# The first norm's factor moved behind the matmul: v from a raw, already transposed x

## The chip, the cores and the metric

One core of a Trainium2 chip runs the whole kernel. The metric is device time in microseconds (us) of one execution; the time before is the median of three runs. A difference under about 0.2% of it (2.4 us) is not told from no change.

## The reference

Two layers of a decoder trunk run over 512 tokens of 1024 channels in float32. Each layer is a mixer, a squared-ReLU MLP and a gated embedding, with an RMSNorm ahead of each and behind each. Layer 0 mixes by attention with a forget gate, layer 1 by a short convolution. The change touches only the beginning of layer 0:

```python
hn   = x * rsqrt(mean(x*x, axis=-1) + 1e-6) * g        # RMSNorm, one factor per token
proj = hn @ w_attn_in                                  # q | k | v | forget-gate logits
log_f = log_sigmoid(proj[..., 3*D:] + b_forget)
c     = cumsum(log_f, axis=1)
s     = q @ k.T / 8 + c[:, None] - c[None, :]          # causal, softmax over keys
m     = softmax(s) @ v @ w_attn_out
```

The factor `r = rsqrt(...)` belongs to a token, and a token is a row of `hn` and of `proj`. So `(x * r) @ w` and `(x @ w) * r` are the same product.

## The kernel before, in words

Every float32 operand of a matmul is split into a high part (rounded to the fast matmul format) and a low part (the rest). A product is then three matmuls: high by high, low by high, high by low (`mm3`, lines 266 to 272). The gain `g` of the first norm is multiplied into the rows of the weights while these are split (`split_gained`, L279: ScalarE writes the high part at L285, VectorE the low part at L287). `prepare(n)` splits weight tiles up to the n-th in a planned order and fetches what it needs into 14 buffers; `wide(...)` calls it eight tiles ahead of the matmul that wants one. Split weights, x and most other blocks are tiles of 128 x 512 in one pool of 70 "pages"; matmul results take one of eight banks of PSUM.

The tokens stand in four blocks t of 128. For attention the norm's result must stand as channels (on the partitions) by tokens, in the pair `hT`. It is made so, for each block: two DMAs load x as tokens by channels (`load_x`); ScalarE and VectorE take the mean square of one half each (L312, L317), GpSimd raises it to the power -1/2 (L692), VectorE multiplies (L698, `n_h`), TensorE turns 2 x 4 squares by a transpose (L337, `n_p`), ScalarE and VectorE split the turned block into `hT` (L276 and L277, for block 0 L723 and L708).

v and the 16 gate logits are made in three column chunks, `V_CHUNKS`: chunk 0 is 272 columns wide (256 of v and the 16 logits), chunk 1 is 512 and chunk 2 is 256. `values(c, t)` makes one chunk of one block with 24 matmuls (8 slices of channels, three matmuls each). Chunk 0 runs by an order written out by hand (`manual_schedule`, lines 716 to 748): twelve matmuls on a constant tile come first (`work(12)`, L1152), and the transposes of the next block stand in the midst of each block's 24 matmuls (L479). Chunks 1 and 2 (L472, with the matmuls at L268 to L270) and everything after have their order set by a planner, that may also place such work between the steps written by hand. `keep_v` adds the gate bias to the logits and splits v out of PSUM (ScalarE L500, VectorE L502). Then come the logs of the gates, their running sum by matmul (`sums_of_logs`, L446, put behind chunk 1 of block 2), its way through DRAM to the score biases (L459, L550), chunk 2, and the projection of q and k from all of `hT` (`project`, from the first matmul on all 512 tokens at once).

All loads go through SyncE's queue in order, apart from half of the first x block and the gains, that go through ScalarE's. The first loads have their order written by hand (lines 1139 to 1147): x block 0, four weight tiles, x block 1, four weight tiles, x blocks 2 and 3, the gate bias.

Of the kernel before, what the change touches and what calls it, by code (L numbers as in the profile page):

```python
# [8 lines left out]
F32 = mybir.dt.float32  # L9
# [6 lines left out]
P = 128  # L16
D = 1024
# [51 lines left out]
def trunk(ctx: ExitStack, tc, x, pT, g, gT, wv, wqk, bf, wo, wci, wcq, cw, wco, wup, wdn, wpp, wpg, out):  # L69
# [308 lines left out]
    def load_x(name, t):  # L378
        xs = [page(f"{name}{t}_{n}") for n in range(2)]
        for n in range(2):  # L380
            eng = nc.scalar if name == "xa" and n else nc.sync
            eng.dma_start(xs[n][:, :S], x[t * P : (t + 1) * P, n * S : (n + 1) * S])
        return xs
# [29 lines left out]
    def attention(hT, first_x, b_f, work, by_hand):  # L413
        vs = [[page(f"v{t}_{i}", F32R) for i in range(4)] for t in range(NB)]
# [46 lines left out]
        def values(c, t, mid=None):  # L461

            c0, width = V_CHUNKS[c]
            n_v = min(width, D - c0)
            ps = bank(f"v{c}_{t}")
            for k in range(KT):
                if width == 256:
                    w = wide("v", c, k // 2).at(lambda u: u[:, k % 2 * 256 : k % 2 * 256 + 256])
                else:
                    w = wide("v", c, k, soon=0 if mid else SOON)  # L470
                if not mid:
                    mm3(ps[:, :width], tokens(hT, k, t), w, k == 0, k == KT - 1)  # L472
            HH, LH, HL = ("hi", "hi"), ("lo", "hi"), ("hi", "lo")
            order = [(u, n) for n in range(2) for u in (HH, HL, LH)] if mid else []
            for i, ((part, of), n) in enumerate(order):
                if i == (5 if t else 3):
                    mid()
                for k in range(4 * n, 4 * n + 4):
                    nc.tensor.matmul(  # L479
                        ps[:, :width], getattr(tokens(hT, k, t), part),  # L480
                        getattr(ready["v", c, k], of),
                        start=k == 0 and part == of, stop=k == KT - 1 and part == "lo",
                    )

            def keep_v():
                if n_v < width:
                    nc.vector.tensor_tensor(
                        out=logit[:, t * H : (t + 1) * H], in0=ps[:, n_v:width], in1=b_f,
                        op=ALU.add,
                    )  # L490
                splits = []
                for c1 in range(0, n_v, 256):
                    src = ps[:, c1 : c1 + 256].rearrange("p (i e d) -> p i e d", e=2, d=HD)
                    block = vs[t][(c0 + c1) // 256].rearrange("p (i r) -> p i r", i=2)
                    for e in range(2):
                        hi = block[:, :, 192 * e : 192 * e + HD]
                        lo = block[:, :, 64 + 64 * e : 128 + 64 * e]
                        splits.append((hi, lo, src[:, :, e, :]))
                for hi, _, src in splits:
                    nc.scalar.copy(hi, src)  # L500
                for hi, lo, src in splits:
# [3 lines left out]

            return keep_v
# [174 lines left out]
        E, done_v = mybir.EngineType, []  # L681
# [13 lines left out]
        def scale_rows(t, r):  # L695
            hs = [page(f"{name}_h{t}_{n}") for n in range(2)]
            for n in range(2):
                nc.vector.tensor_scalar(  # L698
                    out=hs[n][:, :S], in0=first_x[t][n][:, :S], scalar1=r, scalar2=None,
                    op0=ALU.mult,  # L700
                )
            return hs

        quads = lambda ps: ps.rearrange("p (j c) -> p j c", j=4)

        def keep_low(n, ps):
            hi, lo = (u[:, 4 * n : 4 * n + 4, :P] for u in (hT.hi, hT.lo))
            nc.vector.tensor_tensor(  # L708
                out=lo, in0=quads(ps), in1=hi.bitcast(F32), op=ALU.subtract
            )  # L710

        def turn_rows(t, hs):
            for n in range(2):
                keep(t, n, turned(t, n, hs[n], name), hT)

        with tc.manual_schedule(engines={E.PE, E.DVE, E.Activation, E.Pool}):
            work(12)
            r = inverse(0, mean_squares(0))
            prepare(2)
            hs = scale_rows(0, r)  # L720
            prepare(4)
            ps0 = [turned(0, n, hs[n], name) for n in range(2)]
            nc.scalar.copy(hT.hi[:, :4, :P], quads(ps0[0]))  # L723
            v = mean_squares(1)
            keep_low(0, ps0[0])
            prepare(5)
            r = inverse(1, v)
            nc.scalar.copy(hT.hi[:, 4:, :P], quads(ps0[1]))
            hs1 = scale_rows(1, r)
            prepare(KT)  # L730
            keep_low(1, ps0[1])
            v = mean_squares(2)
            r = inverse(2, v)
            done_v.append(values(0, 0, lambda: turn_rows(1, hs1)))
# [545 lines left out]
```

## Time and profile before

| | us |
|---|---|
| median of 3 runs | 1221.15 |
| lowest, highest | 1221.05, 1221.59 |
| the profiled execution | 1220.75 |
| its span, first to last instruction | 1219.0 |
| TensorE busy | 1208.5 |
| VectorE busy | 919.2 |
| ScalarE busy | 684.0 |
| GpSimd busy | 653.8 |
| read from HBM | 136.93 MB |

In rows of the profile PE is TensorE's matmuls, PEld its weight loads, DVE VectorE, ACT ScalarE, POOL GpSimd, SP SyncE; a q behind a name is that engine's queue of DMA issues and waits. A timeline row holds the start, the time from the first start to the last end, engine, line, operation, tiles (written <- read), and a count where like instructions in a row are merged. Matmuls overlap: the distance of two starts, not the length of one, is what one costs. A group's row holds busy time and the mean of one in ns. A table by windows gives each engine's busy time in each stretch.

### The profile page before, as it was taken

The page shows a single profiled execution, that of the slowest core. Times are in us where ns is not written, and L with a number is a line of the kernel's source. Part 1 is how long each engine was busy: PE and PEld are TensorE (multiplying, and loading weights), DVE is VectorE, ACT ScalarE, POOL GpSimd, SP SyncE. Part 2 cuts the span into 40 slices and gives each one's busy share as a digit, 9 for nine tenths or more (in the row PEclk, how much of TensorE's full clock was granted, in tenths as well). Part 3 has the DMA queues.
Part 4 walks back from the last instruction along what each step waited for, and adds up shares of the span by engine and source line. Part 5 has one row for each costly group of instructions (what it writes and reads, how often), then busy time and mean ns, then how long its engine had stood idle before and what let it go on. Part 6 is the DMA issues. An engine that isn't in the chain of part 4 may idle for free.

```text
span 1219.0 us, 18773 instructions
## 1 busy us (share of the span) xinstructions
PE 1208.5 (99%) x6202; PEld 1030.3 (85%) x6202; DVE 919.2 (75%) x1466; ACT 684.0 (56%) x1457; POOL 653.8 (54%) x612
## 2 busy tenths in 40 slices
PE   9999999999999999999999999999999999999997
PEld 7888887898888888888889999989888888888886
DVE  7668889576769766879877788766876787669873
ACT  5567778458634563455666433545756445635551
POOL 1036667154787777775213355226676878678210
PEclk9999999999999999999999999999999999999999
DMA  8555555623244223438223123552422443235401
GB/s 277 168 151 164 166 142 134 216 88 95 87 121 138 87 73 119 138 88 284 73 91 114 28 86 104 164 164 70 138 84 60 134 139 100 64 113 176 169 12 58
DMA packets 86162, 148.74 MB, mean 122 GB/s; under 512 B 10224, under 2 KB 17952, under 8 KB 86064
## 3 DMA queue, kind: packets, MB, share of 16 engines
q1 hardware_dynamic: 85488, 147.01, 39.3%
q8 instruction: 49, 0.80, 0.3%
q10 hardware_dynamic: 576, 0.53, 0.1%
q14 instruction: 49, 0.40, 0.1%
HBM read 136.93 MB, written 6.37 MB: 118 GB/s over the span
## 4 chain that ended last, share of the span: by engine, by line
PE 92%; issue 2%; DVE 2%; ACT 2%; POOL 1%; DMA 0%; POOLq 0%; DVEq 0%; ACTq 0%
PE up L268 9%; PE up L270 9%; PE up L269 9%; PE dn L268 8%; PE dn L270 8%; PE dn L269 8%; PE qk L270 2%; PE qk L269 2%; PE qk L268 2%; PE pg L268 2%; PE pg L270 2%; PE pg L269 2%; PE pT L579 1%; PE co L269 1%; PE co L268 1%
## 5 line engine op out<-in xcount | busy, mean ns | idle before, releaser
L277 DVE TENSOR_TENSOR wl<-raw,wh 128x512 fp32r<-128x512 f32 x346 | 344.8, 1042 | 14.4 <-ACT wh L276 13.5
L269 PE MATMUL up<-hTh,wl 128*128 128x512 f32 (+1 forms) x576 | 210.2, 365 | 0.0
L270 PE MATMUL up<-hTl,wh 128*128 128x512 f32 (+1 forms) x576 | 209.6, 365 | 0.0
L268 PE MATMUL up<-hTh,wh 128*128 128x512 f32 (+1 forms) x576 | 208.7, 366 | 0.0
L276 ACT CAST wh<-raw 128x512 fp32r<-128x512 f32 x346 | 189.8, 626 | 4.5 <-DVE xd L373 4.4
L940 ACT ACTIVATE r<-up 128x512 f32<-128x512 f32 (+1 forms) x72 | 39.6, 550 | 202.2 <-PE up L270 180.9
L277 POOL TENSOR_TENSOR wl<-dn_T,wh 128x512 fp32r<-128x512 f32 x96 | 132.1, 1410 | 30.1 <-ACT wh L276 30.1
L168 POOL TENSOR_TENSOR dn_T<-raw,raw 128x512 f32<-128x512 f32 x56 | 87.3, 1570 | 69.1 <-DMA raw<-in_wdn 49.1
L269 PEld LDWEIGHTS up<-hTh,wl 128*128 128x128 f32 x576 | 108.6, 188 | 17.5
L268 PEld LDWEIGHTS up<-hTh,wh 128*128 128x128 f32 x576 | 108.6, 188 | 17.5
L270 PEld LDWEIGHTS up<-hTl,wh 128*128 128x128 f32 x576 | 108.2, 188 | 17.6
L986 DVE TENSOR_TENSOR acc<-dn,acc 128x512 f32<-128x512 f32 x168 | 107.4, 679 | 14.9 <-PE dn L270 14.8
L168 POOL TENSOR_TENSOR dn_T<-raw,dn_T 128x512 f32<-128x512 f32 x56 | 92.3, 1648 | 2.2
L276 ACT CAST wh<-dn_T 128x512 fp32r<-128x512 f32 x112 | 61.5, 618 | 10.9 <-POOL dn_T L168 10.9
L277 DVE TENSOR_TENSOR A12l<-q,A12h 128x512 fp32r<-128x512 f32 x28 | 22.0, 787 | 53.9 <-ACT A12h L276 53.9
L1000 POOL TENSOR_TENSOR acc<-acc,acc 128x512 f32<-128x512 f32 x28 | 46.9, 1708 | 9.9 <-DVE acc L986 9.9
L270 PE MATMUL qk<-hTl,wh 128*128 128x512 f32 x128 | 50.8, 397 | 0.0
L269 PE MATMUL qk<-hTh,wl 128*128 128x512 f32 x128 | 50.8, 397 | 0.0
L268 PE MATMUL qk<-hTh,wh 128*128 128x512 f32 x128 | 50.7, 396 | 0.0
L269 PE MATMUL pg<-wh,hTl 128*128 128x512 f32 x128 | 50.5, 394 | 0.0
L268 PE MATMUL pg<-wh,hTh 128*128 128x512 f32 x128 | 50.4, 394 | 0.0
L270 PE MATMUL pg<-wl,hTh 128*128 128x512 f32 x128 | 50.2, 392 | 0.0
(404 smaller groups left out, 3274.3 us busy)
## 6 DMA issues: line engine op xcount, KB each, us to landing
raw<-in_wup SPq DMA_DIRECT2D x128, 256.0 KB, 2.9
raw<-in_wdn SPq DMA_DIRECT2D x128, 256.0 KB, 2.9
raw<-in_wcq SPq DMA_DIRECT2D x36, 256.0 KB, 2.8
raw<-in_wqk SPq DMA_DIRECT2D x32, 256.0 KB, 3.4
raw<-in_wpg SPq DMA_DIRECT2D x32, 256.0 KB, 4.1
g<-in_g SPq DMA_DIRECT2D x22, 256.0 KB, 5.4
prl<-neg_c SPq DMA_DIRECT2D x16, 256.0 KB, 6.7
raw<-in_wo SPq DMA_DIRECT2D x16, 256.0 KB, 5.8
```

The lines of the kernel that those rows point to most:

```text
L168: ins = nc.gpsimd.tensor_tensor(out=B[name], in0=B[a], in1=B[b], op=op)
L268: nc.tensor.matmul(ps, a.hi, b.hi, start=start, stop=False)
L269: nc.tensor.matmul(ps, a.lo, b.hi, start=False, stop=False)
L270: nc.tensor.matmul(ps, a.hi, b.lo, start=False, stop=stop)
L276: nc.scalar.copy(hi, src)
L277: return eng.tensor_tensor(out=lo, in0=src, in1=hi.bitcast(F32), op=ALU.subtract)
L579: nc.tensor.transpose(ps[:, b * P : (b + 1) * P], probs[h][b][:, j * P : (j + 1) * P], ident)
L940: nc.scalar.activation(r[:, :n], ps[:, :n], AF.Relu)
L986: ins = nc.vector.tensor_tensor(out=a, in0=banks[s], in1=a, op=ALU.add)
L1000: nc.gpsimd.tensor_tensor(out=a, in0=a, in1=acc[i, s][:, :S], op=ALU.add)
```

## The change

x goes into the kernel a second time, laid out on the host as channels by tokens (`xT`, 2 x 128 x 512 for each block). Its eight tiles are loaded first and split into high and low as they are. Chunk 0 is made from these raw pairs, in half blocks (`part`, 12 matmuls each), and chunk 1 too; the token's factor `rs[t]` is multiplied in when v and the logits are taken out of PSUM (`keep_values`). The x laid out as tokens by channels is now loaded after `xT`, and only its mean squares are taken. Chunk 2 and the projection of q and k still read the normed `hT`. To make that, the factors of a block are written to DRAM, and read back as a row on every partition (`rows_of`); GpSimd multiplies the raw `xT` tiles by this row (`normed_x`), and ScalarE and VectorE split the product into `hT`. The scaling by VectorE, the 32 transposes and the splits out of PSUM go. Nine constant matmuls stand ahead instead of twelve, and the pages of v are taken when they are written.

```diff
-        vs = [[page(f"v{t}_{i}", F32R) for i in range(4)] for t in range(NB)]
+        vs = [[None] * 4 for t in range(NB)]
...
+        def split_x(t, n):
+            turned[t, n] = Pair(*(page(f"x{s}{t}_{n}", F32R) for s in "hl"))
+            split(turned[t, n].hi[:, :S], turned[t, n].lo[:, :S], raw_x[t][n][:, :S])
...
+        def part(ps, t, n):
+            for p, of in ("hi", "hi"), ("hi", "lo"), ("lo", "hi"):
+                for k in range(4 * n, 4 * n + 4):
+                    nc.tensor.matmul(
+                        ps[:, : V_CHUNKS[0][1]], getattr(of_x(k, t), p),
+                        getattr(ready["v", 0, k], of),
+                        start=k == 0 and p == of, stop=k == KT - 1 and p == "lo",
+                    )
...
+            for hi, _, src in splits:
+                if c < 2:
+                    nc.scalar.mul(hi, src, rs[t])
...
+            for hi, lo, src in splits:
+                if c < 2:
+                    nc.vector.scalar_tensor_tensor(
+                        out=lo, in0=src, scalar=rs[t], in1=hi.bitcast(F32),
+                        op0=ALU.mult, op1=ALU.subtract,
+                    )
...
+        def rows_of(t):
+            nc.sync.dma_start(r_T[t : t + 1, :].rearrange("o p -> p o"), rs[t])
+            nc.sync.dma_start(
+                r_row[:, t * P : (t + 1) * P], r_T[t : t + 1, :].partition_broadcast(P)
+            )
+        def normed_x(t):
             for n in range(2):
+                h = raw_x[t][n][:, :S].rearrange("p (j c) -> p j c", j=4)
+                r = r_row[:, t * P : (t + 1) * P].unsqueeze(1).to_broadcast([P, 4, P])
+                nc.gpsimd.tensor_tensor(out=h, in0=h, in1=r, op=ALU.mult)
+                to = lambda u: u[:, 4 * n : 4 * n + 4, t * P : (t + 1) * P]
+                split(to(hT.hi), to(hT.lo), h)
+        banks_v = [bank(f"v0_{t}") for t in range(NB)]
         with tc.manual_schedule(engines={E.PE, E.DVE, E.Activation, E.Pool}):
-            work(12)
-            r = inverse(0, mean_squares(0))
...
+            work(9)
+            split_x(0, 0)
+            prepare(4)
+            part(banks_v[0], 0, 0)
+            split_x(0, 1)
+            split_x(1, 0)
+            part(banks_v[1], 1, 0)
+            prepare(KT)
+            part(banks_v[0], 0, 1)
+            split_x(1, 1)
+            part(banks_v[1], 1, 1)
+            for t in (2, 3):
+                for n in range(2):
+                    split_x(t, n)
+                    part(banks_v[t], t, n)
+            for t in range(2):
+                rs[t] = inverse(t, mean_squares(t))
+                prepare(KT + 2 * t + 2)
+            prepare(2 * KT)
+            for t in range(2):
+                keep_values(0, t, banks_v[t])
+            for t in (2, 3):
+                rs[t] = inverse(t, mean_squares(t))
+                keep_values(0, t, banks_v[t])
+        for t in range(NB):
+            rows_of(t)
...
         for t in range(NB):
-            values(1, t)()
+            values(1, t)
+            normed_x(t)
             if t == 2:
                 sums_of_logs(tri)
...
-        first_x = [load_x("xa", 0)]
+        raw_x = [[page(f"xT{t}_{n}") for n in range(2)] for t in range(NB)]
+        for n, eng in enumerate((nc.sync, nc.scalar)):
+            eng.dma_start(raw_x[0][n][:, :S], xT[0, n])
         nc.scalar.dma_start(first_g, gT)
         fetch(4)
-        first_x.append(load_x("xc", 1))
-        fetch(KT)
+        for t in range(1, NB):
+            for n in range(2):
+                nc.sync.dma_start(raw_x[t][n][:, :S], xT[t, n])
+            if t == 1:
+                fetch(KT)
+        first_x = [load_x("xc", t) for t in range(2)]
+        fetch(RAWS)
         first_x += [load_x("xc", t) for t in (2, 3)]
```

More of the change, by code (lines that the diff above doesn't have):

```diff
@@ L380, in load_x @@
         for n in range(2):
[L381 to L382 removed]
+            nc.sync.dma_start(xs[n][:, :S], x[t * P : (t + 1) * P, n * S : (n + 1) * S])
         return xs
@@ L469, in values @@
                 else:
[L470 to L482, printed above, removed]
-                    )
@@ L485, in keep_v @@
[L485 to L501, printed above, removed]
+                    w = wide("v", c, k)
@@ L712, in turn_rows @@
-        def turn_rows(t, hs):
-            for n in range(2):
-                keep(t, n, turned(t, n, hs[n], name), hT)
+        r_T = dram.tile([NB, P], F32, tag="r_T", name="r_T")
+        r_row = page("r_row")
+        def rows_of(t):
[4 more added lines that the diff above has]
+        def normed_x(t):
+            for n in range(2):
+                h = raw_x[t][n][:, :S].rearrange("p (j c) -> p j c", j=4)
[3 more added lines that the diff above has]
+                split(to(hT.hi), to(hT.lo), h)
```

84 lines of the change are left out of this document (33 added, 51 removed).

## The prediction

> **What bounds the kernel now.** I read the page first: engines, slices, chain. Then a table by windows of the first 59 us, since the change touches nothing later.
>
> ```profile
> PE 1208.5 (99%) x6202; PEld 1030.3 (85%) x6202; DVE 919.2 (75%) x1466; ACT 684.0 (56%) x1457; POOL 653.8 (54%) x612
> ...
> PE 92%; issue 2%; DVE 2%; ACT 2%; POOL 1%; DMA 0%; POOLq 0%; DVEq 0%; ACTq 0%
> ```
>
> ```profile
> 0.00:13.00 13.00, 10.10 (x49) 7.91 (x49) 8.48 (x22) 8.96 (x20) 1.83 (x9) 1.00 0.86 250
> 13.00:30.00 17.00, 17.00 (x117) 16.01 (x118) 13.88 (x35) 8.82 (x22) 2.19 (x4) 1.00 0.85 298
> 30.00:47.40 17.40, 17.40 (x81) 13.98 (x81) 13.48 (x45) 10.58 (x34) 0.00 (x0) 1.00 0.56 170
> 47.40:59.00 11.60, 11.60 (x98) 11.60 (x97) 5.51 (x18) 5.16 (x18) 2.31 (x7) 1.00 0.51 157
> ```
>
> TensorE is busy 99% and carries 92% of the chain of waits. In the window rows (PE, PEld, DVE, ACT, POOL busy, clock, DMA share, GB/s) it never rests from 13 us on; it rests only in the first 13 us. So a matmul that goes, or an earlier start, moves everything behind it, provided nothing else runs late. VectorE is the next engine: 13.48 of 17.40 us just before chunk 2. The stage, in TensorE's starts:
>
> ```profile
> 1.50 4.81 PE L1152 MATMUL warm_p<-warm 128*128 128x512 f32 x12 [1.50 <-DVE warm L1138]
> 7.12 1.09 PE L337 MATMUL n_p<-ident,n_h 128*128 128x128 f32 x8 [0.81 <-DVE n_h L698]
> ...
> 13.55 0.66 PE L479 MATMUL v<-wh,hTh 128*128 128x272 f32 x4
> 14.05 0.66 PE L479 MATMUL v<-wl,hTh 128*128 128x272 f32 x4
> ...
> 16.05 1.04 PE L337 MATMUL n_p<-ident,n_h 128*128 128x128 f32 x8
> 16.85 0.74 PE L479 MATMUL v<-wh,hTl 128*128 128x272 f32 x4
> ...
> 37.30 0.39 PE L268 MATMUL v<-wh,hTh 128*128 128x512 f32 x1
> ...
> 37.98 0.39 PE L268 MATMUL v<-wh,hTh 128*128 128x512 f32 x1
> ...
> 40.70 0.40 PE L446 MATMUL ps_c<-tri,lf_h 128*16 128x512 f32 x1
> ...
> 41.87 0.44 PE L268 MATMUL v<-wh,hTh 128*128 128x512 f32 x1
> ...
> 47.40 0.28 PE L268 MATMUL v<-wh,hTh 128*128 128x256 f32 x1
> ...
> 58.91 0.40 PE L268 MATMUL qk<-hTh,wh 128*128 128x512 f32 x1
> ```
>
> Four matmuls of 272 columns cost 0.50 us (13.55 to 14.05), 0.125 each: chunk 0, 96 of them, is 12.0 us. Three of 512 cost 0.68 (37.30 to 37.98): chunk 1, again 96, is 21.8. Eight transposes cost about 0.8 (16.05 to 16.85). The sums of logs take 1.17 (40.70 to 41.87). Chunk 2 starts at 47.40, after chunks 0 and 1, and takes 11.5 (47.40 to 58.91). I compute when the new kernel reaches chunk 2; the difference to 47.40 is the gain.
>
> **The change, part by part.** Durations:
>
> ```profile
> L276 ACT CAST wh<-raw 128x512 fp32r<-128x512 f32 x346 | 189.8, 626 | 4.5 <-DVE xd L373 4.4
> L285 ACT ACTIVATE wh<-raw,first_g 128x512 fp32r<-128x512 f32 x8 | 5.5, 733 | 0.0
> L287 DVE SCALAR_TENSOR_TENSOR wl<-raw,first_g,wh 128x512 fp32r<-128x512 f32 x8 | 5.8, 748 | 0.4
> L287 DVE SCALAR_TENSOR_TENSOR wl<-raw,first_g,wh 128x256 fp32r<-128x256 f32 x40 | 16.6, 481 | 0.2
> L277 DVE TENSOR_TENSOR wl<-raw,wh x346: 674/684/1789, 159.6 to 1177.5; 128x512 fp32r<-128x512 f32 x173
> L317 DVE CUSTOM_DVE_ANT_0 n_q_sq<-xc 128x512 f32<-128x512 f32 x3 | 2.1, 686 | 0.0
> L502 DVE TENSOR_TENSOR v<-v,v 128x128 fp32r<-128x128 f32 x32 | 7.3, 280 | 11.5 <-ACT v L500 11.4
> L168 POOL TENSOR_TENSOR dn_T<-raw,raw 128x512 f32<-128x512 f32 x56 | 87.3, 1570 | 69.1 <-DMA raw<-in_wdn 49.1 <-DVE acc L986 6.2 <-DVE wl L277 4.1
> ```
>
> *Removed on TensorE:* 32 transposes, 32/8 x 0.8 to 0.9 = 3.5 us, and the waits between them. *Moved earlier:* the first product waits no more for mean square, power, scaling, transpose and split, only for load and split. The rows of the start:
>
> ```profile
> 4.31 0.63 ACT L312 ACTIVATE junk<-xa 128x512 f32<-128x512 f32 x1 [1.31 <-DMA xa<-in_x]
> 5.19 1.77 ACT L285 ACTIVATE wh<-raw,first_g 128x272 fp32r<-128x272 f32 x4 [0.16 <-DMA first_g<-in_gT]
> 5.75 0.92 DVE L287 SCALAR_TENSOR_TENSOR wl<-raw,first_g,wh 128x272 fp32r<-128x272 f32 x2 [0.29 <-ACT wh L285]
> ...
> 8.93 0.52 ACT L285 ACTIVATE wh<-raw,first_g 128x272 fp32r<-128x272 f32 x1
> ```
>
> The first `xT` tile lands as x did, 4.3; its high part is out at 4.9, its low part at 5.6. ScalarE splits the first four weight tiles by 6.96 as now, VectorE (0.46 each) by 7.6; half block (0,0) ends near 8.25 and (1,0) near 9.75. Weights 4 to 7 come no sooner than now (their high parts begin at 8.93 today and end after 11, with other work between; four alone take 1.77, and I take 10.8 for the last, 11.3 for its low part). Half (0,1) then ends near 12.0; five more halves of 1.5 (12 x 0.125) follow, (1,1) to (3,1), whose splits, eight of 0.63 on ScalarE and 0.68 on VectorE, are done before each. Chunk 0 ends at 12.0 + 5 x 1.5 = 19.5.
>
> *The loads.* One more MB stands ahead of chunk 1's weights, and x blocks 2 and 3 are put ahead of the last two of these.
>
> ```profile
> 9.13 0.55 SPq L158 DMA_DIRECT2D raw<-in_wv  x1
> ```
>
> ```profile
> raw<-in_wv SPq DMA_DIRECT2D x1, 256.0 KB, 5.7
> ```
>
> ```profile
> 16.00:18.00 2.00, 2.00 (x19) 2.00 (x18) 1.20 (x5) 1.31 (x3) 1.23 (x3) 1.00 1.04 396
> ```
>
> Today the first tile of chunk 1 is issued at 9.13 and lands 5.7 later, 14.8. At 396 GB/s (the DMA engines are full there) a tile of 256 KB takes 0.66. With four x tiles more ahead it lands at 17.5, the sixth at 20.8, and behind four further x tiles the last two at 24.1 and 24.8. Split at 0.73 and 0.75, the last pair is whole at 26.4. TensorE, on chunk 1 from 19.5, wants the seventh tile at 23.6 and would end the first block at 25.0. In strict order it ends at 26.6: a stall of 1.6. If the planner draws the second block's matmuls forward, 0. For that the trace has half a case: today the planner puts chunk 1's first matmuls before the last block of chunk 0, but it plans by its own estimate of the landings. I take the middle, 0.8.
>
> *Sum.* 19.5 + 21.8 + 1.2 + 0.8 = 43.3: chunk 2 starts 4.1 us earlier than at 47.40. Bounds: 4.9 without the stall, 3.3 with it all.
>
> *Added beside TensorE, costed at nothing there:* the factors. VectorE takes block 3's mean square after the weights and the first evictions, near 30; the row then needs a write and a read through DRAM, in SyncE's queue, where the read waits for its write and the weight loads for q and k wait behind both (TensorE asks for these tiles only after chunk 2, near 54). The near rows are small transfers and a DRAM round trip:
>
> ```profile
> L797 SPq DMA_DIRECT2D taps<-in_cw x1: 328/328/328, 16.9 to 16.9; - x1
> ...
> DMA to landing us min/median/max: 4.9/4.9/4.9
> ```
>
> ```profile
> L459 SPq DMA_DIRECT2D neg_c<-neg_c x4: 306/342/357, 43.5 to 45.3; - x4
> ...
> DMA to landing us min/median/max: 1.4/5.6/9.7
> ```
>
> Twice 4.9 (the nearest in size and place) puts the last row at 40.5; between twice 1.4 and twice 9.7 it lies from 33 to 50. GpSimd's two multiplies of 1.6 and a split (0.6, 0.7) make block 3 of `hT` ready at 45, from 38 to 54. It is wanted by its part of chunk 2, at 43.3 + 3/4 x 11.5 = 51.9. So the cover is 7 us, and at the worst end 2 us are lost. VectorE: the scalings (8 of 0.48) and eight splits out of PSUM go, sixteen splits of 0.68 come, so 1.6 us more, and the evictions of v keep their form (7.3/32 = 0.23). From 26.4 to 51.9 I count 25 us of work for it (24 evictions 5.5, two mean squares 1.8, 16 half tiles of weights at 16.6/40 = 0.42, 6.6, eight splits of `hT` 5.5, and by estimate 5.5 for logits, logs and running sums, some twenty short instructions): full, but about 8 us of it (half those weights, the last evictions, the running sums) aren't wanted before 54. ScalarE gets eight more splits of 0.63, 5 us, and has 10.58 of 17.40 today. Hence no cost, as long as its instructions keep their length.
>
> That is the weak place. The low-part subtraction shows 684 ns as median and 1789 as longest, over a kernel in which GpSimd is 54% busy; between 13 and 47 us today GpSimd has 2.19 us of work, and the weights' split with its two SBUF inputs (L287) keeps to 748. The change puts 8 x 1.57 = 12.6 us of GpSimd multiplies there. Between nothing and 12.6 us of lengthening I take about half, 6 us, inside the cover. The Trainium skill, "SBUF — State Buffer", section "SBUF: two separate sides", says that a VectorE operation with two SBUF inputs and a GpSimd operation lock each other out for a whole instruction. By that rule the higher end is possible, and it speaks against the change; by the sum above it is covered. The 1789 agrees with it, no row here proves it.
>
> *Fewer warm matmuls.* Twelve fill 1.50 to 6.31. In that stretch eight fill 3.38 to 6.31, so they go faster towards the end; nine would end near 5.5, and until 9.8 TensorE would be half busy with 24 matmuls of 0.125. If it ran at half pace there, 24 x 0.125 = 3.0 us of extra work falls on waits of about 1.5 us: cost 0 to 1.5. I take 0: today, too, it is idle for 0.81 after the warm matmuls and waits several times before 13 us, and at 13.55 matmuls are 0.125 apart.
>
> ```profile
> 3.38 2.93 PE L1152 MATMUL warm_p<-warm 128*128 128x512 f32 x8
> ```
>
> "TensorE: Matmul & The Clock Gate" of the Trainium skill, section "Part 1: The HAM clock gate", has the clock halved again after an idle window of about 3.4 us; TensorE has no such gap here, so it too gives 0.
>
> **The rivals.** *A, forecast:* 1220.75 (the profiled execution, span 1219.0 and 1.75 around it) - 4.1 = 1216.65; the median of the runs lies 0.40 above that execution, so 1217.0. With the bounds of the stall and some drift in the planner's order 1215.5 to 1218.5.
>
> *B, no change to be told:* the full stall of 1.6, the 1.5 of half pace, together 3.1 off 4.9: gain 1.8, 1219.3. For it: the strict order is plausible, the weights land late by the loads' own rows. Against: both must come.
>
> *C, slower:* VectorE becomes the bound. If every GpSimd multiply holds it up in full, 12.6 us join the 17 that can't wait, and with 4 of the 8 postponable ones put ahead the last split of `hT` falls at 26.4 + 17 + 12.6 + 4 = 60, that is 8.1 after 51.9; less the gain of 4.1 it is 4 slower, 1225. It decides where `hT` comes at 56.0 (no gain left), and is told from no change at 58.4. For it: the 1789 ns and the full 25 us. Against: the planner puts `hT` ahead of what can wait, and VectorE is half idle after 47 today (5.51 of 11.60).
>
> *D, the transposes cost nothing today:* excluded by the window rows, TensorE doesn't rest from 13 on.
>
> **How the numbers follow.** A 0.64, B 0.17, C 0.19. Faster by over 0.2% (2.4 us) 0.65, within 0.17, slower 0.18. A alone spans 1215.5 to 1218.5; to leave out no more than 2 in 10 the range takes in B and the start of C: 1214.8 to 1221.8.
>
> **What would show it.** In the profile after: the first product on x near 5.8, no `n_p` rows, the last 272-column matmul near 19.5, the first 256-column matmul of chunk 2 near 43.3, the first qk matmul near 54.8; chunk 1's seventh weight tile landing near 24 with a gap on TensorE of up to 1.6; `hT` splits of block 3 done by 45 and none waited for by TensorE; VectorE's subtractions between 0.7 and 1.8 us beside GpSimd's multiplies. I am wrong if TensorE waits on `hT` in chunk 2 (C), on weights longer than 1.6, or if the order after 59 us changes.

## The result and the profile after

The changed kernel takes 1239.63 us (median; 1237.98 to 1240.59) against 1221.24 for the kernel before: a ratio of 1.0149, 95% interval 1.0131 to 1.0166. It is 18 us slower, where 4 us faster was forecast. The profiled execution is one of 1239.36 us, with a span of 1237.6. A trace shows one execution, in the runs below up to 3 us from its kernel's median, so starts and waits are compared in traces and times by medians.

| start on TensorE, us | before | predicted | after |
|---|---|---|---|
| first product on x | 13.55 | near 5.8 | 5.87 |
| chunk 1 (first 512-column matmul) | 22.33 | 19.5 | 19.61 |
| sums of logs | 40.70 | (not given) | 51.22 |
| chunk 2 (first 256-column matmul) | 47.40 | 43.3 | 59.17 |
| q and k | 58.91 | 54.8 | 71.20 |
| scores | 75.26 | (not given) | 90.41 |

The page of the kernel after, engines and then the chain of waits by engine:

```profile
PE 1208.8 (98%) x6167; PEld 1028.7 (83%) x6167; DVE 935.5 (76%) x1466; ACT 690.0 (56%) x1465; POOL 668.8 (54%) x620
...
PE 85%; DMA 5%; DVE 4%; issue 2%; ACT 2%; POOL 1%; SPq 0%; POOLq 0%; DVEq 0%; ACTq 0%
```

TensorE's work didn't grow (1208.5 before), it waits: its share of the chain fell from 92% to 85%, and DMAs, that had 0%, have 5%. The table by windows of the kernel after, cut as in the prediction (PE, PEld, DVE, ACT, POOL busy, clock, DMA share, GB/s), and one window more:

```profile
13.00:30.00 17.00, 17.00 (x101) 15.21 (x100) 11.06 (x26) 9.55 (x20) 1.59 (x2) 1.00 1.11 355
30.00:47.40 17.40, 6.13 (x28) 4.74 (x26) 6.43 (x22) 5.26 (x13) 3.32 (x5) 0.80 0.39 99
47.40:59.00 11.60, 7.78 (x30) 6.02 (x31) 10.78 (x11) 10.82 (x29) 10.25 (x8) 0.71 0.24 81
...
71.20:90.40 19.20, 16.51 (x74) 13.35 (x73) 13.42 (x35) 11.16 (x24) 6.44 (x8) 1.00 0.74 208
```

From 30 to 47.4 us every engine is idle for most of the time: TensorE works 6.13 of 17.40 us, VectorE 6.43, the DMAs move 99 GB/s. So no engine is full there; something is waited for. Then VectorE needs 10.78 us for 11 instructions, while GpSimd is busy 10.25. TensorE's timeline of the kernel after (start, length, line, tiles, wait before):

```profile
5.87 1.63 PE L473 MATMUL v<-wh,xh 128*128 128x272 f32 x4 [0.16 <-ACT wh L285]
...
19.61 0.40 PE L268 MATMUL v<-wh,xh 128*128 128x512 f32 x1
...
35.75 0.39 PE L270 MATMUL v<-wl,xh 128*128 128x512 f32 x1
51.22 0.61 PE L445 MATMUL ps_c<-tri,lf_h 128*16 128x512 f32 x1 [15.09 <-ACT lf_h L276]
...
54.15 0.40 PE L268 MATMUL v<-wh,xh 128*128 128x512 f32 x1
...
59.17 0.33 PE L268 MATMUL v<-wh,hTh 128*128 128x256 f32 x1
...
71.20 0.40 PE L268 MATMUL qk<-hTh,wh 128*128 128x512 f32 x1
...
90.41 0.30 PE L581 MATMUL sc<-kh,qs 128*128 128x128 f32 x1 [2.70 <-DMA kh<-kh]
91.72 0.47 PE L582 MATMUL sc<-kl,qs 128*128 128x128 f32 x1 [1.01 <-DMA kl<-kl]
```

The first 36 us went as forecast. At 35.98 (35.75 and one pitch of 0.23) 72 of chunk 1's 96 matmuls were through. The other 24 (5.4 us) and the sums (1.2) would have brought chunk 2 to 42.6, 4.8 ahead of 47.40. But the sums of logs stood next in TensorE's order, and their logs came at 51.2. The account against before: -4.8 for the start; +15.2 for this gap; +1.3 since the seven matmuls behind it ran at half pace (51.22 to 54.15, 2.93 us for 7 x 0.23 = 1.6); +0.5 in chunk 2; +2.9 from q and k to the scores (19.2 us for 16.35), with the 2.7 us wait for the keys' transfers in it; +3.4 behind that. Together 18.5; the spans differ by 18.6. Of the last 3.4, 1.0 is the second wait for the keys, and about 1.5 the clock behind it (granted 0.50 from 92 to 94 us and 0.74 from 94 to 96); the rest is not traced.

Why the logs were late is in the queues. SyncE's, in the kernel after, and below it the time to landing of the four writes of factors (view of `n_r`) and of the four reads (view of `r_row`):

```profile
24.86 0.38 SPq L717 DMA_DIRECT2D r_T<-n_r  x1
...
26.29 0.39 SPq L717 DMA_DIRECT2D r_T<-n_r  x1
27.54 8.14 SPq L158 DMA_DIRECT2D raw<-in_wqk  x6
35.77 1.32 SPq L717 DMA_DIRECT2D r_T<-n_r  x2
37.78 8.56 SPq L718 DMA_DIRECT2D r_row<-r_T  x4
46.87 0.81 SPq L158 DMA_DIRECT2D raw<-in_wqk  x2
```

```profile
DMA to landing us min/median/max: 9.4/9.9/10.0
```

```profile
DMA to landing us min/median/max: 4.7/6.4/8.4
```

A write takes 10 us, the last two leave at 35.8, and their reads hold the queue until 46.3: no load for q and k is issued between 35.7 and 46.9. What stood behind the row on the other engines of the kernel after:

```profile
46.28 9.94 POOL L726 TENSOR_TENSOR xT<-xT,r_row 128x512 f32<-128x512 f32 x7 [11.25 <-DMA r_row<-r_T]
...
48.22 1.08 DVE L277 TENSOR_TENSOR hTl<-xT,hTh 128x512 fp32r<-128x512 f32 x1 [8.89 <-ACT hTh L276]
49.23 1.28 DVE L436 SCALAR_TENSOR_TENSOR logf<-logit,f_l 128x64 f32<-128x64 f32 x1
...
50.93 0.24 ACT L276 CAST lf_h<-logf 128x64 fp32r<-128x64 f32 x1 [0.61 <-DVE logf L436]
```

On VectorE the planner had put the first split of `hT` ahead of the last step of the logs. So VectorE waited 8.89 us for GpSimd's product, and the last step of the logs, whose inputs were there at 38.9 (`f_l`; the logits at 34), waited with it. In the kernel before, the same step, with a cast and a step of the logs to compare lengths with:

```profile
31.73 0.41 DVE L757 CAST tri<-ones 128x512 fp32r<-128x512 f32 x1
32.06 0.21 DVE L434 TENSOR_TENSOR f_r<-f_r,f_ru 128x64 f32<-128x64 f32 x1
...
34.15 0.22 DVE L437 SCALAR_TENSOR_TENSOR logf<-logit,f_l 128x64 f32<-128x64 f32 x1
```

### The profile page after: what moved, and what is told of

It is laid out like the page before. It is cut to its first block, busy times and chain, and to the rows that moved or that the text cites. A ratio compares the mean times of both kernels' runs of the same rounds, so it can differ in the third digit from the quotient of the medians.

```text
span 1237.6 us, 18749 instructions
## 1 busy us (share of the span) xinstructions
PE 1208.8 (98%) x6167; PEld 1028.7 (83%) x6167; DVE 935.5 (76%) x1466; ACT 690.0 (56%) x1465; POOL 668.8 (54%) x620
## 3 DMA queue, kind: packets, MB, share of 16 engines
q1 hardware_dynamic: 87792, 149.37, 38.9%
## 4 chain that ended last, share of the span: by engine, by line
PE 85%; DMA 5%; DVE 4%; issue 2%; ACT 2%; POOL 1%; SPq 0%; POOLq 0%; DVEq 0%; ACTq 0%
PE up L270 9%; PE up L269 9%; PE up L268 9%; PE dn L268 8%; PE dn L269 8%; PE dn L270 8%; PE qk L270 2%; PE qk L269 2%; PE qk L268 2%; PE pg L269 2%; PE pg L268 2%; PE pg L270 2%; DMA raw<-in_wqk 2%; PE pT L597 1%; PE co L269 1%
## 5 line engine op out<-in xcount | busy, mean ns | idle before, releaser
L277 DVE TENSOR_TENSOR wl<-raw,wh 128x512 fp32r<-128x512 f32 x346 | 349.2, 1054 | 14.3 <-ACT wh L276 13.5
L1009 POOL TENSOR_TENSOR acc<-acc,acc 128x512 f32<-128x512 f32 x28 | 46.9, 1709 | 9.9 <-DVE acc L995 9.9
L287 DVE SCALAR_TENSOR_TENSOR wl<-raw,first_g,wh 128x256 fp32r<-128x256 f32 (+2 forms) x88 | 46.1, 571 | 5.7 <-ACT wh L285 5.4
```

The lines of the kernel that those rows point to most:

```text
L277: return eng.tensor_tensor(out=lo, in0=src, in1=hi.bitcast(F32), op=ALU.subtract)
L287: eng.scalar_tensor_tensor(out=lo[:, c], in0=src[:, c], scalar=first_g[:, k : k + 1], in1=hi[:, c].bitcast(F32), op0=ALU.mult, op1=ALU.sub ...
L1009: nc.gpsimd.tensor_tensor(out=a, in0=a, in1=acc[i, s][:, :S], op=ALU.add)
```

## The experiments

Theory 1 after this reading: the row's 10 us writes and its place in SyncE's queue are the cost. Rivals: GpSimd's multiplies stretch VectorE; the order in which the queues hold logs, chunk 1 and splits; or the new stage is late however the row comes.

### One cause at a time

**The writes alone, in the kernel before** (nobody reads them):

```diff
+        for t in range(NB):
+            nc.sync.dma_start(r_T[t : t + 1, :].rearrange("o p -> p o"), rs[t])
```

> Edit: the kernel before, with four writes of the factors to DRAM in pieces of 4 bytes added in SyncE's queue; nobody reads them. This prices the write by itself. Theory 1: each write lands 5 to 10 us after its issue and the weight loads behind it in the queue land up to 5 us later each; the time stays within 0.3% of 1221.2, since the loads have slack there. If a small write costs what the gate bias's or the taps' small loads cost, it lands in 2 to 5 us and nothing behind it moves.

1221.36 us, ratio 1.0002 (0.9993 to 1.0012). The writes take 9.7 to 11.0 us to land here too and cost nothing that can be told: only what waits for them is dear.

**The row made on TensorE** from diagonals of the factors, in place of the round trip:

```diff
-            nc.sync.dma_start(r_T[t : t + 1, :].rearrange("o p -> p o"), rs[t])
...
+            nc.scalar.mul(d.hi[:, :P], ident, rs[t])
...
+            nc.tensor.matmul(ps[:, :P], warm[:, :P], d.hi[:, :P], start=True, stop=False)
+            nc.tensor.matmul(ps[:, :P], warm[:, :P], d.lo[:, :P], start=False, stop=True)
+            nc.scalar.copy(r_row[:, t * P : (t + 1) * P], ps[:, :P])
```

> Edit: the row of factors is no longer written to DRAM in 128 pieces of 4 bytes and read back; a diagonal of the factors is multiplied by ones on TensorE (two 128-column matmuls a block) and copied out by ScalarE. GpSimd's eight multiplies stay. Theory 1 (the round trip through DRAM is what is late; the sums of logs and chunk 2 only wait behind it): no wait of 15 us at the sums of logs, chunk 2 starts at 42 to 44 instead of 59.2, the time is 1216 to 1219. Theory 2 (GpSimd's multiplies stretch VectorE, the forecast's rival C): the multiplies are still there, so the wait moves little and the time stays above 1230.

1239.27 us, ratio 1.0148 (1.0133 to 1.0163): theory 1 missed by 20 us. TensorE's timeline of this kernel:

```profile
35.46 0.47 PE L724 MATMUL r_ps<-rd_h,warm 128*128 128x128 f32 x1 [14.83 <-ACT rd_h L718]
...
40.78 0.73 PE L268 MATMUL v<-wh,xh 128*128 128x512 f32 x1
```

The round trip is gone and the gap is as long, only earlier: the planner put these matmuls ahead of all of chunk 1, which now starts at 40.78, and their diagonals come late on ScalarE.

**No row to wait for**: it is set to ones, so that chunk 2, q and k lack the factor.

```diff
-            nc.sync.dma_start(r_T[t : t + 1, :].rearrange("o p -> p o"), rs[t])
...
+            if t == 0:
+                nc.vector.memset(r_row[:, :S], 1.0)
```

> Edit: the round trip is left out, the row is set to ones (the factor is left out of the normed x for chunk 2, q and k); the multiplies, splits and orders stay the planner's. Theory 1: chunk 2 starts at 42 to 43, the time is 1216 to 1218, a bound for any cure of the row. Theory 2: above 1230.

1230.40 us, ratio 1.0073 (1.0058 to 1.0088). Half of the loss goes and half stays without any late row. TensorE still waits 11.5 us for the logs. From this kernel's timeline, VectorE while GpSimd multiplies (34.6 to 45.2), and TensorE's start of the sums:

```profile
35.86 1.53 DVE L763 CAST tri<-ones 128x512 fp32r<-128x512 f32 x1
37.32 1.28 DVE L429 SCALAR_TENSOR_TENSOR f_r<-f_u,f_e 128x64 f32<-128x64 f32 x1
...
41.36 1.28 DVE L433 TENSOR_TENSOR f_r<-f_r,f_ru 128x64 f32<-128x64 f32 x1
...
47.11 0.61 PE L445 MATMUL ps_c<-tri,lf_h 128*16 128x512 f32 x1 [11.47 <-ACT lf_h L276]
```

The multiplication of `f_r` that takes 0.21 us before takes 1.28, the cast 1.53 for 0.41: each ends within 0.3 us behind the end of a GpSimd multiply (1.3 us apiece). The Trainium skill, "SBUF — State Buffer", section "SBUF: two separate sides", has the pair of ports held for a whole instruction, also against VectorE operations in a two-port mode; these rows agree with it.

**A row of ones, multiplied on VectorE** instead of GpSimd:

```diff
-                nc.gpsimd.tensor_tensor(out=h, in0=h, in1=r, op=ALU.mult)
+                nc.vector.tensor_tensor(out=h, in0=h, in1=r, op=ALU.mult)
```

> Edit on the kernel with the row of ones (factor left out of chunk 2, q and k): the eight multiplies by the row move from GpSimd to VectorE. With the row of ones the logs still took 13 us, from 34 to 47, each of VectorE's short steps 1.3 to 1.5 us long beside a GpSimd multiply. If GpSimd holds VectorE up (theory 2), the short steps go back to 0.2 to 0.5, the logs are done by 41, the wait at the sums falls from 11.9 to 4 to 6, and the time is 1221 to 1225 against 1230.4. If the late statistics or the order alone make the wait, it stays at 10 to 12 and 1229 or more.

1239.16 us, ratio 1.0148 (1.0133 to 1.0163). The time missed, the lengths came as expected: without GpSimd's multiplies the cast takes 0.42 us again and the multiplication of `f_r` 0.22. But the sums start at 56.91, after a wait of 20.4 us for the logs, since the planner put multiplies and splits ahead of them on VectorE. So GpSimd is not the only way to be late; the order is one of its own.

**The logs ahead of the splits** on VectorE (first), and on VectorE and ScalarE (second, shown), the round trip kept:

```diff
-            split(lf.hi, lf.lo, logf)
+            logs_done.append(nc.scalar.copy(lf.hi, logf))
+            logs_done.append(nc.vector.tensor_tensor(
+                out=lf.lo, in0=logf, in1=lf.hi.bitcast(F32), op=ALU.subtract
+            ))
...
-                split(to(hT.hi), to(hT.lo), h)
+                behind(nc.scalar.copy(to(hT.hi), h), logs_done[0])
+                behind(nc.vector.tensor_tensor(
+                    out=to(hT.lo), in0=h, in1=to(hT.hi).bitcast(F32), op=ALU.subtract
+                ), logs_done[1])
```

> Edit: the round trip stays; the first split of the normed x on VectorE is ordered behind the last step of the logs. Theory 1: the 15 us wait at the sums of logs goes, but TensorE then waits at chunk 2 for the normed x, which comes at about 49 as before: chunk 2 at 49 to 50 instead of 59.2, time 1229 to 1232. Theory 3 (only VectorE's order is at fault, the late row would be hidden): chunk 2 at 42 to 44, time 1216 to 1219. Theory 2: VectorE is still stretched, 1235 or more.

1240.47 us, ratio 1.0157 (1.0140 to 1.0174). That is in theory 2's range, but not by its cause: VectorE's logs are done at 39.7, and on ScalarE their high part stood behind the first cast of `hT`, which waits for the row: the sums start at 50.70. The cure moved the wait to the next queue.

> Edit on the changed kernel: the splits of the normed x are ordered behind the logs' last split, on VectorE and on ScalarE too (in e3 ScalarE's queue still held the logs' high part back behind the first cast of the normed x, to 50.4). The round trip stays. If order in the queues makes the 15 us wait: the high part is out by 40 to 41, the wait at the sums is 4 to 5. Then the late row shows by itself: the first block of the normed x is ready at 49 to 50, chunk 2 starts there and not at 42.6, its last block's split comes at 58 or later; time 1228 to 1232. If the late row were hidden without the order: 1220 to 1224.

1237.22 us, ratio 1.0127 (1.0112 to 1.0142); TensorE's waits in it:

```profile
PE ps_c L450 <- ACT lf_h L441: 4.8, 1, 4.8
PE v L269 <- DVE hTl L734: 4.4, 2, 2.5
```

The sums start at 41.07 and chunk 2 at 50.21, as expected; the time is 5 us above the expected range. Now chunk 2 waits for `hT` and the scores for the keys, and of 9 us won at chunk 2 only 2.4 arrive in the median.

**The sums of logs behind chunk 1's fourth block** (`if t == 3` for `if t == 2`):

> Edit on the changed kernel: the sums of logs are asked for behind chunk 1's fourth block instead of its third, so 24 matmuls (5.45 us) more stand ahead of the waiting one in TensorE's queue; nothing else. If the logs come late whatever TensorE does (the high part of the logs at 50.9), the wait of 15.2 falls to 9.8, chunk 2 starts at 53 instead of 59.2 and the time is 1233 to 1235. If TensorE's order alone were at fault, the time is below 1222.

1238.59 us, ratio 1.0145 (1.0130 to 1.0160). The wait shrinks to 9.2 us as expected, but one of 4.9 follows for the logs' low part, and q and k start at 70.6, 0.6 earlier: the expected 1233 to 1235 us don't come, nothing is won beyond the interval.

### A ladder, with the orders mended

Three kernels have the logs first on both engines and the sums last. The first leaves the norm's path out; the second adds the multiplies, the third the row through DRAM:

```diff
+            if t == 0:
+                nc.vector.memset(r_row[:, :S], 1.0)
...
-                nc.gpsimd.tensor_tensor(out=h, in0=h, in1=r, op=ALU.mult)
...
-            if t == 2:
+            if t == 3:
```

> The norm's path is left out: the row is ones, nobody multiplies by it and nothing goes through DRAM, so chunk 2, q and k take x without the factor (this leaves out part of the computation); the splits of x stand behind the logs on VectorE and ScalarE, and the sums of logs behind the fourth block of chunk 1. Theory (the loss comes only from getting the factor to the splits): TensorE has no gap above 1.5 us between 19.6 and q and k, chunk 2 starts at 42 to 44, the first scores at 70 to 72.5, 1216 to 1219 us. Rival (the mean squares and evictions put off to 26 to 34 us are enough to lose it): a gap of 4 us or more before the sums of logs or chunk 2 stays, first scores behind 75, 1221 us or more.

> The same with GpSimd's eight multiplies by the row of ones put back (the factor itself is still left out of chunk 2, q and k). Theory (beside a GpSimd multiply a VectorE operation takes 0.5 to 1 us longer, and 13 us of multiplies fall on the logs and splits): chunk 2 starts 2 to 6 us later than in the run without multiplies, 1220 to 1228 us. Rival (the multiplies are hidden once the row is early and the logs go first): within 1.5 us of the run without them.

> The same with the row's round trip through DRAM put back: the changed kernel, with the logs ahead of the splits on both engines and the sums of logs last. Theory (round trip of 10 us a write and 46 to 51 us for the row): the wait before the sums is gone, one of 4 to 8 us before chunk 2's first block takes its place, and the first scores wait 2 to 3 us for the keys behind the delayed loads; 1230 to 1236 us. Rival (with both engines' order mended the row's lateness is covered): 1220 to 1226 us.

1225.38, 1231.07 and 1236.62 us; ratios 1.0034 (1.0022 to 1.0047), 1.0078 (1.0063 to 1.0093), 1.0127 (1.0112 to 1.0143). So, in medians, +4.4 us with the norm's path to `hT` left out, +5.7 with GpSimd's multiplies, +5.6 with the row through DRAM, and the last 3.0 to the changed kernel with the planner's orders. The last step of the logs on VectorE without and with the multiplies (first and second kernel, nothing else differs):

```profile
40.18 0.22 DVE L438 SCALAR_TENSOR_TENSOR logf<-logit,f_l 128x64 f32<-128x64 f32 x1
```

```profile
47.11 0.21 DVE L438 SCALAR_TENSOR_TENSOR logf<-logit,f_l 128x64 f32<-128x64 f32 x1
```

VectorE has the same steps in the same order ahead of it in both; they are stretched, it comes seven us later, and TensorE waits 5.9 us for it. The lock is thus measured, for multiplies that fall on the logs. In the third kernel the row comes late: the multiplies begin at 46.1, the sums start at 41.39 without a wait, and instead chunk 2 waits 6.3 us for `hT` and the scores 4.8 for the keys. So the steps of the ladder are not shares of the changed kernel's loss; the second's 5.7 are not in the third.

The first rung is the surprise: chunk 2 starts at 42.7 and q and k at 55.3, 3.6 us ahead of before, and it is still slower, at a place that neither theory had named. In its TensorE timeline:

```profile
77.03 0.44 PE L586 MATMUL sc<-kh,qs 128*128 128x128 f32 x1 [5.21 <-DMA kh<-kh]
```

The scores wait for the transfers that double the keys, and behind the wait the granted clock is 0.50 until 81 us, some 2 us more. Windows of the kernel before, then of this one:

```profile
20.00:40.00 20.00, 20.00 (x106) 17.29 (x105) 17.64 (x52) 15.95 (x44) 0.00 (x0) 1.00 0.74 229
40.00:60.00 20.00, 20.00 (x137) 18.14 (x136) 9.55 (x35) 6.83 (x26) 2.49 (x8) 1.00 0.46 148
60.00:72.00 12.00, 12.00 (x55) 9.93 (x54) 5.35 (x13) 5.13 (x12) 0.14 (x1) 1.00 0.52 147
```

```profile
20.00:40.00 20.00, 19.92 (x87) 15.82 (x87) 12.79 (x39) 11.02 (x27) 2.93 (x5) 1.00 0.74 254
40.00:60.00 20.00, 19.42 (x133) 17.33 (x132) 20.00 (x59) 19.67 (x59) 0.47 (x1) 1.00 0.43 115
60.00:72.00 12.00, 11.82 (x53) 9.45 (x51) 8.68 (x19) 5.81 (x13) 4.89 (x7) 1.00 0.79 235
```

VectorE does 5 us less from 20 to 40 us (in that stretch of the first rung it waits 3.5 us for weights that ScalarE splits late, since their loads land behind x by tokens, and 3.4 us in turns with ScalarE and GpSimd for the factors and evictions), and is full from 40 to 60, where it had 9.55. ScalarE likewise. The loads for q and k, whose buffers come free by VectorE's splits, move from that stretch into the next (235 GB/s for 147), where the keys' transfers are issued: in the median they land after 5.1 us instead of 2.7.

### Chunk 2 from raw x too

Now only q and k need the normed x, 12 us later. With the late row (through DRAM, GpSimd's multiplies, logs first, sums last):

```diff
-                mm3(ps[:, :width], of_x(k, t) if c == 1 else tokens(hT, k, t), w, k == 0, k == KT - 1)
+                mm3(ps[:, :width], of_x(k, t), w, k == 0, k == KT - 1)
...
-                if c < 2:
+                if c < 3:
```

> The changed kernel with its row through DRAM and GpSimd's multiplies, the logs first and the sums of logs last, and chunk 2 from raw x. Theory (the row in place at 46 to 51 us and multiplies until 58 to 62 are too late for q and k at 55 too): chunk 2 starts at 42.5 to 44 without a wait, q and k wait 4 to 8 us, the scores a little more behind delayed loads; 1224 to 1230 us. Rival (12 us more are enough for it): waits below 2 us in all, 1217 to 1221 us.

1236.24 us, ratio 1.0128 (1.0114 to 1.0142). Slower than either case. Chunk 2 starts at 42.47, but then stops for 10.7 us:

```profile
62.90 0.58 PE L268 MATMUL v<-wh,xh 128*128 128x256 f32 x1 [10.68 <-DVE c_T L455]
```

It needs the bank of PSUM that held the sums, and VectorE's copy out of that bank (at 62.2) stood behind seven splits of `hT` that wait for the row's products, from 48.9 on. Whatever shares a queue with the consumers of the late row is late too.

Before that the same idea had been tried with the row on TensorE behind chunk 1's second block, blocks 2 and 3's mean squares earlier, the logs first and the sums last, but chunk 2 from the normed x:

> Edit on the changed kernel, all causes taken away together: the mean squares of blocks 2 and 3 come ahead of chunk 1's last two weights and of the evictions, the row is made on TensorE (behind chunk 1's second block), the splits of the normed x stand behind the logs, the sums of logs behind chunk 1. GpSimd's multiplies stay. If these causes are all: no wait over 2 us on TensorE, chunk 2 at 42.6 to 44.5, time 1216 to 1218.5. If the lock between GpSimd and VectorE alone is enough for a loss: 1221 or more.

1236.16 us, ratio 1.0122 (1.0105 to 1.0139), 18 us above what was expected if its edits removed every cause: TensorE waits 12.0 us for the first diagonal, which ScalarE makes at 43 behind weights and evictions. With the diagonals in the order written by hand, and chunk 2 from raw x:

```diff
-            prepare(2 * KT)
-            for t in range(2):
-                keep_values(0, t, banks_v[t])
+            prepare(KT + 6)
             for t in (2, 3):
...
+            for t in range(NB):
+                diagonal(t)
```

> Chunk 2 too is made from raw x, so that only q and k need the factor in x; the row is made on TensorE from diagonals of the factors behind the third block of chunk 1, and GpSimd multiplies behind the logs. Theory (the loss is lateness against the first use of the normed x, which is now 12 us later): no gap above 3 us before chunk 2, which starts at 42 to 45; q and k at 55 to 59; 1215 to 1222 us. Rival (the multiplies and the work of evictions put VectorE and ScalarE behind whatever the use): q and k at 62 or later, 1224 us or more.

1225.44 us, ratio 1.0030 (1.0017 to 1.0044). The diagonals are there at 32, chunk 2 starts at 43.4, and TensorE's waits from 15 to 95 us come to:

```profile
PE qk L268 <- ACT hTh L753: 2.7, 1, 2.7
PE qk L270 <- DVE hTl L754: 0.5, 1, 0.5
```

So 14 of the 18 us are recovered, and the 4 us of head start at chunk 2 are spent at q and k, behind GpSimd's multiplies (45 to 58 us). Next the multiplies on VectorE, and then the row's matmuls allowed one block earlier (`last_mm[1]` for `last_mm[2]`):

> Chunk 2 from raw x and the row from TensorE as in the run before, with the eight multiplies on VectorE behind the logs instead of on GpSimd. Theory (beside GpSimd the operations of VectorE are stretched, so without GpSimd the eight multiplies cost VectorE 4.5 to 5.5 us and the rest runs at its own pace): the gaps of 3.0 and 1.1 us before q and k are gone or below 1.5 us together, q and k at 54.8 to 57, 1216 to 1221 us. Rival (VectorE is full either way): q and k at 58 or later, 1222 to 1227 us.

> The same with the row's eight matmuls let in behind the second block of chunk 1 instead of the third. Theory: the row is in place at 33 to 38 instead of 45 us and the splits of x are done before q and k need them; no gap above 1 us before q and k at 54.8 to 56; the scores at 71.5 to 74; 1215.5 to 1220 us. Rival (the earlier multiplies go ahead of evictions and weights on VectorE): a gap of 2 us or more before chunk 2, and 1220 to 1226 us.

1225.02 and 1226.02 us; ratios 1.0033 (1.0021 to 1.0045) and 1.0038 (1.0026 to 1.0051). q and k start at 54.77 and 54.64, over 4 us ahead of before, and it doesn't last: 2.6 and 1.4 us go on `hT`, and then, as in the first rung, 3.1 and 3.8 us on the keys. So the expected 1216 to 1221 us were missed each time by waits behind the place that was mended. The second edit moved nothing: the row's first matmul starts at 41.07, against 41.19 without it, since the planner left it behind all of chunk 1. So no run with chunk 2 from raw x had its row before 45 us, and expectations that count on one at 33 to 38 us were not put to the test.

### Another queue for the keys

```diff
-                            nc.sync.dma_start(h[b, :S].bitcast(F32), h[a, :S].bitcast(F32))
+                            nc.scalar.dma_start(h[b, :S].bitcast(F32), h[a, :S].bitcast(F32))
```

With the multiplies on VectorE, on GpSimd, and in the kernel before:

> The run with the early row and VectorE's multiplies, with the transfers that double the keys on ScalarE's queue instead of SyncE's. Theory (SyncE's order holds the keys): they land about 3 us after their issue, the scores start at 71.5 to 73.5 without a wait above 1 us, 1217 to 1221.5 us. Rival (VectorE is late with the splits of the keys themselves, or the transfers share the same full DMA engines): a wait of 2.5 us or more for the keys stays, 1223 us or more.

> The same with the multiplies on GpSimd instead of VectorE. Theory (with the row at 35 to 38 us the multiplies end by 50): q and k at 55 to 57 with less than 2 us of waits, scores at 72 to 75, 1217 to 1222 us. Rival (the multiplies stretch VectorE's evictions and splits as before): waits of 3 us or more before q and k, 1223 us or more.

> The kernel before with the transfers that double the keys on ScalarE's queue: the control. Its scores start without a wait for the keys, so 1220 to 1222 us (no change) by either theory; if the queue alone gains, 1219 us or less.

1229.02, 1229.80 and 1228.89 us; ratios 1.0060 (1.0047 to 1.0074), 1.0067 (1.0055 to 1.0080) and 1.0065 (1.0052 to 1.0077). The control is slower by 7.9 us, by neither theory: the queue itself is dear (the last section), so these times can't tell what SyncE's order costs. What can be read is when the keys' high parts go out and how long they take to land, with VectorE's multiplies before the move and after it:

```profile
L561 SPq DMA_DIRECT2D kh<-kh x4: 467/480/528, 69.3 to 79.7; - x4
...
DMA to landing us min/median/max: 2.9/5.1/6.2
```

```profile
L561 ACTq DMA_DIRECT2D kh<-kh x4: 468/468/517, 69.6 to 82.7; - x4
...
DMA to landing us min/median/max: 3.2/5.3/6.7
```

```profile
PE sc L589 <- DMA kh<-kh: 3.2, 1, 3.2
```

ScalarE's queue sent the first key no sooner (69.6 for 69.3): ScalarE stood still for 6.0 us there, until a load of weights had landed. The first key lands after 6.2 and 6.7 us, and TensorE waits as long as before the move. In the kernel before it goes out at 65.2, 0.6 us behind the start of its cast, and lands in 2.4 us. In the first rung of the ladder it goes out 7.5 us behind its cast (61.0), since seven loads for q and k stand ahead of it in SyncE's queue, and takes 8.4 us:

```profile
59.73 8.30 SPq L158 DMA_DIRECT2D raw<-in_wqk  x7
68.50 0.72 SPq L558 DMA_DIRECT2D kh<-kh  x1
```

So the keys go out late, behind the postponed loads, and they land slowly, beside them; no run parts the two. That the postponement comes from VectorE's full stretch, 40 to 60 us, is read from the windows; no run took away the second copy of x or the raw splits to show it. No version tried here beats the kernel before; the nearest are 0.3% behind.

## Why the prediction was wrong, step by step

- *The start.* Right. The first product on x came at 5.87 (near 5.8 given), chunk 1 at 19.61 (19.5). Nine warm matmuls instead of twelve cost nothing, as taken.
- *The loads.* The stall on chunk 1's last weights, taken at 0.8, was 0: the last pair was whole at 26.4, as forecast (the terms given, 24.8 + 0.73 + 0.75, add up to 26.3), and the planner drew the second block forward. The gain before the gap was 4.8, the better bound.
- *"Added beside TensorE, costed at nothing there: the factors."* This step failed. Its cover of 7 us was counted against one consumer, block 3's part of chunk 2 at 51.9. In VectorE's order the first split that waits for the row's product stood ahead of the last step of the logs, and in TensorE's the sums of logs stood ahead of the rest of chunk 1. So the cover ran out at 36, when TensorE asked for the sums; the row's first part came at 46.2, the sums started at 51.22, and 15.2 us were lost there. The text counted the logs among what can't wait and didn't ask what they stand behind. With the logs put first on both engines 4.8 us of this wait stayed, and the late row was waited for at chunk 2.
- *The round trip, twice 4.9 us.* Mis-sized: writes 10 us, reads 4.7 to 8.4. The two rows it was taken from were transfers of other forms; for a write in 128 pieces of 4 bytes the trace had no like. The last row, put at 40.5 and at 50 at the worst, landed at 50.7: its factors were there at 33.9 and not near 31, its write stood 2.6 us in the queue and took 9.4, its read 4.7. The last split of `hT`, bounded by 54, began at 69.1.
- *The lock, "about half, 6 us, inside the cover".* The mechanism was right. The size is near what the ladder gives (the logs 6.9 us later and the kernel 5.7 slower), but that is with a row that is there from the start. In the changed kernel the multiplies ran from 46.3 to 57.7 and met only the last step of the logs, beside weights and splits; what they cost there was not measured alone. The cover was not there.
- *SyncE's queue.* Named, and called harmless since q and k's tiles are wanted at 54. But no load went out from 35.7 to 46.9, and later the keys' first transfer stood behind seven loads in that queue (issued at 82.7, 5.8 us behind its cast; 0.6 in the kernel before): waits of 2.7 and 1.0 us at the scores. That the order behind 59 us might change stood in the last sentence as a way to be wrong, without a price.
- *The clock.* The half pace was asked only of the start. After 15.1 us without work it cost 1.3 us. "TensorE: Matmul & The Clock Gate" of the Trainium skill, "Part 1: The HAM clock gate", halves the clock after an idle window of about 3.4 us; the pitch of 0.43 us behind the gap agrees.
- *Rival C* had the sign and one of the causes, at 1225. It let VectorE's fullness fall on the last block of `hT` alone; the traces show it at the logs and at `hT`, and suggest it at a third place, the loads that its splits set free.

## What to carry to other kernels

A late value costs at every queue in which something useful stands behind one of its consumers, so its slack is counted to the first such instruction on each engine and not to the first matmul that reads it. Mending one queue shows the next: before spending runs on single cures, leave the whole suspected path out once, and see whether anything is to be won (here nothing was: without the norm's path to `hT` the kernel was still 4.4 us slower). Work that an engine doesn't do in a stretch in which it waits for data can return as a backlog later, and with it the loads whose buffers that engine sets free. And look in the trace whether an edit that only allows another order has changed the order.

## What was not expected of the hardware

- A write of 128 factors to DRAM in pieces of 4 bytes took 9.4 to 11.0 us to land, in the kernel before as in the one after. The Trainium skill, "DMA: Bandwidth & Descriptors", section "Specifications", says that pieces under 512 bytes are read, modified and written; it names no price, and no run here shows the mechanism.
- Beside GpSimd's multiplies even VectorE operations on 128 x 64 elements went from 0.21 to 1.28 us, about the length of a whole GpSimd multiply (1.3 us). The reciprocal of one input kept its 0.54 us in the first and the second rung of the ladder.
- Issuing the keys' transfers from ScalarE made the kernel before 7.9 us slower. ScalarE's waits from 80 to 195 us in it (the row in the kernel before read 0.8 us, once):

```profile
ACT kh L276 <- DVE kl L277: 7.6, 5, 1.6
```

ScalarE, which issues the transfers there, waits itself for what they need (here VectorE's low part), and the casts queued behind wait too. The loss does fall in this stretch: the scores start at 75.2 in both kernels, the output projection at 198.7 instead of 191.8. That these waits make all of it was not tried.
